# Rounded-float32 matmuls that read their moving operand as two interleaved strands

## The chip, the cores and the metric

One core of a Trainium2 chip runs one program. The metric is the device time in microseconds; the median of three runs is shown, with the span of one profiled execution. The engines are TensorE (PE; its weight loads, PEld, are listed apart), VectorE (DVE), ScalarE (ACT), GpSimd (POOL) and the queue of SyncE (SP), which issues most transfers.

## The reference

Two layers over 512 positions of width 1024, float32. Layer 0 mixes with a Conformer convolution module, layer 1 with native sparse attention; each mixer is followed by a SwiGLU FFN of inner width 2816. The branches of the reference for other mixers do not run at this depth.

```python
D_MODEL = 1024; SEQ = 512; DEPTH = 2; D_FF = 2816

def swiglu_ffn(h, w_in, w_out):
    gate, up = jnp.split(h @ w_in, 2, axis=-1)
    return (jax.nn.silu(gate) * up) @ w_out

def reference(x, ...):
    for i in range(DEPTH):
        h = rmsnorm(x, norm_mix[i])
        if m == 0:   y = conformer_conv_module(h, ...)   # GLU, 31-tap depthwise conv, LayerNorm, SiLU, projection
        elif m == 1: y = nsa_attention(h, ...)           # 16 heads of 64: compressed, selected and window branch
        x = x + y
        h = rmsnorm(x, norm_ffn[i])
        x = x + swiglu_ffn(h, ffn_w_in[i], ffn_w_out[i])
    return x
```

## The kernel before

**Layout.** Activations lie transposed: `x[m]` is a tile of 128 features by 512 tokens (P = 128, T = 512, H = 256), eight of them. A projection multiplies a 128x128 block of weights (stationary, loaded for each matmul) with such a tile (moving, 512 columns) into one PSUM bank.

**Three matmuls a product.** For accuracy each factor is split into a rounded-float32 high part (type `F32R`) and the rounded remainder, and a product is the sum of three matmuls, high by high, high by low and low by high. `mm3` (L320) does that for the projections. ACT makes a high part by a copy that rounds, DVE the low part by a subtraction: `w_hi`/`w_lo` for the weights (tiles `wh`, `wl`), `split_x` (L347) for the activations with the norm's gain (`hh`, `hl`), `divide` and `row_part` for the FFN's inner rows (`ah`, `al`, `row`), `out_parts` for the attention's output (`oh`, `ol`). All of these are stored with the tokens in order and read in order.

**The FFN.** A head of projections over 512 columns is followed by 18 pairs (`pair`) that multiply 2x2 blocks with seven products (Winograd's form) instead of eight: the token axis is halved, so that the moving operands have H = 256 columns. They lie in `ball`, made from `z` by `operand_z`, `operand_t`, `operand_h`, `operand_l`, `operand_th` and `operand_tl` during the head (per chunk of features and per high or low part, 256, 512 and 1024 elements) and later from the FFN's inner rows by `block`. The stationary side is made of sums of weight blocks (`sh`, `sl`, or `wh`, `wl` unsummed). `product` (L1013) issues 12 matmuls for one of the seven products. Then come 14 rows of the second projection in plain form (`row_mm`, 512 columns) and four more pairs (`out_pair`).

**The rest.** The attention's scores (`S`) have keys as the moving operand, 128 to 512 columns wide; the probabilities are transposed by matmuls against an identity in plain float32 (`T<-cc,Pm`) and multiplied with the values (`O<-t,v`, plain float32 too). In the V projection (`v_mm`) the roles are swapped: the tokens `hh`, `hl` are stationary and the weights (304 or 256 columns) are moving. The norms sum squares by matmuls against a column of ones (`ssq`, one column). `warm` (L339) issues bf16 matmuls on zeros while TensorE would wait. The convolution's statistics row `rows` (L679) is read from PSUM through `by_phase`, with a step of eight tokens; the first two key tiles are multiplied into `kr` by `norm_x` (L1752) in another order of tokens, the others (`kraw`) in place.

**Order.** The program's order on each engine is the order in which the code is written, with small parts hung on hooks between matmuls; nearly everything is pinned to it. All instructions of the helper classes carry line 153, so the profile's groups are told apart by tile names.

Of the kernel before, what the change touches and what calls it, by code (L numbers as in the profile page):

```python
# [19 lines left out]
P = 128  # L20
# [142 lines left out]


@with_exitstack
def trunk(ctx: ExitStack, tc: tile.TileContext, A, out):
# [228 lines left out]
    def proj_start(pool, tag, xh, xl, hooks=None, pre=None, into=None):  # L395
# [6 lines left out]
        for i in range(4):  # L402
            wh, wl = next_w()
            for k2 in range(2):
                k = 2 * i + k2
                if pre and k + 1 < NK:
                    pre(k + 1)
                if k == 0 and pre:
                    for w, z in ((wh, xh), (wl, xh), (wh, xl)):
                        for m in range(4):  # L410
                            held(nc.tensor.matmul(pss[m], w[:, m * P:(m + 1) * P], z[0], start=w is wh and z is xh,
                                                  stop=False))
# [25 lines left out]
    def conv_module():  # L438
        acc = new_acc()
        with ExitStack() as cx:  # L440
# [53 lines left out]
            for k in range(NK):  # L494
# [8 lines left out]
                if k == 0:  # L503
                    load_tables()
                    for w, z in ((wh, hh), (wl, hh), (wh, hl)):
                        for m in range(2):
                            held(nc.tensor.matmul(pend[m], w[:, m * P:(m + 1) * P], z[0], start=w is wh and z is hh,
                                                  stop=False))
                    continue
                for m in range(2):  # L510
                    c = slice(k % 2 * 256 + m * P, k % 2 * 256 + (m + 1) * P)
                    for w, z in ((wh, hh), (wl, hh), (wh, hl)):
                        held(nc.tensor.matmul(pend[m], w[:, c], z[k], start=False, stop=z is hl and k == NK - 1))
            for k in range(NK):
# [293 lines left out]
            def ln_mul(i):  # L808
# [5 lines left out]
                ah.append(box["a"][0][:, i, :])  # L814
                for z in (ah[i], lny[i]):
                    pe(nc.scalar.activation(z, vch[i], AF.Silu, scale=v(V_LNG + i), bias=v(V_LNB + i)))

            def ln_low(i):
                al.append(box["a"][1][:, i, :])
                pe(nc.vector.tensor_tensor(al[i], lny[i], ah[i], ALU.subtract))  # L820

# [28 lines left out]
    def ffn(acc, gnext, layer, between=None):  # L850
# [12 lines left out]
        with ExitStack() as cx:  # L863
# [20 lines left out]
            def split_last(part):  # L884
                m, g = NK - 1, v(gcol + NK - 1)
                if part == 0:
                    hh[m] = hps[0].tile([P, T], F32R, tag=f"hh{m}", name=nm(f"hh{m}"))
                    hl[m] = hps[0].tile([P, T], F32R, tag=f"hl{m}", name=nm(f"hl{m}"))
                    nc.scalar.activation(hh[m], x[m], AF.Copy, scale=g)
                else:  # L890
                    nc.vector.scalar_tensor_tensor(hl[m], x[m], g, hh[m], ALU.mult, ALU.subtract)

            ah, al, ys = {}, {}, {}

            def divide(f, pool):
                ah[f] = pool.tile([P, T], F32R, tag=f"ah{f}", name=nm("ah"))
                al[f] = pool.tile([P, T], F32R, tag=f"al{f}", name=nm("al"))
                held(nc.scalar.activation(ah[f], ys[f], AF.Copy))
                held(nc.vector.tensor_tensor(al[f], ys[f], ah[f], ALU.subtract))

# [51 lines left out]
            def operand_h(c):  # L952
                z, zt = ops[c]
                nc.scalar.activation(bh[c][:, :H], z[:, :H], AF.Copy, scale=-1.0)
                nc.scalar.activation(bh[c][:, H:3 * H], z[:, T:], AF.Copy)

            def operand_l(c):
                z, zt = ops[c]
                nc.vector.scalar_tensor_tensor(bl[c][:, :H], z[:, :H], -1.0, bh[c][:, :H], ALU.mult, ALU.subtract)
                nc.vector.tensor_tensor(bl[c][:, H:3 * H], z[:, T:], bh[c][:, H:3 * H], ALU.subtract)  # L960
# [198 lines left out]
            def row_part(f):  # L1159
# [204 lines left out]
    def nsa(acc, cosT, sinT, gnext):  # L1364
# [70 lines left out]
        def qk_bc(C, y2, scale=1.0):  # L1435
# [5 lines left out]
            nc.gpsimd.memset(ys[64:].bitcast(F32), 0.0)  # L1441
            nc.scalar.activation(ys[:64], py[:64], AF.Copy, scale=scale)
            nc.vector.scalar_tensor_tensor(ys[32:64], py[32:64], scale, ys[32:64], ALU.mult, ALU.subtract)
            return ys

        def qk_bcast(c, y):
            bc = p2.tile([P, T], F32, tag="p2", name=nm("bc"))
            pe(nc.tensor.matmul(bc, C["er"][c], y, start=True, stop=True))
            return bc
# [39 lines left out]
        def gain(e, ps):  # L1489
# [15 lines left out]
        def square(e, ps):  # L1505
            sqs[e] = (qk.tile([P, T], F32, tag="q2", name=nm("qsq"), bufs=Q2B) if e in (4, 5) else
                      kp.tile([P, T], F32, tag="qsq", name=nm("qsq"), bufs=SQB))
            nc.scalar.activation(sqs[e], ps, AF.Square)

# [40 lines left out]
        def seq16(t):  # L1550
            return t.rearrange("p (n q) -> p n q", q=16)

        later = []

# [29 lines left out]

        def split_1(q, eng):

            hi, lo = (qk.tile([P, T], F32R, tag="q2", name=nm(z), bufs=Q2B) for z in ("qh", "ql"))
            if eng is nc.scalar:
                eng.activation(hi, q, AF.Copy)
            else:  # L1590
                eng.tensor_copy(hi, q)
            nc.gpsimd.tensor_tensor(lo, q, hi, ALU.subtract)
            return hi, lo

        def k_move(c):
            box["k2", c] = split_1(ks[c], nc.scalar)

# [81 lines left out]
        def q_pair(p):  # L1679
# [46 lines left out]
            def trans():  # L1726
# [4 lines left out]
                pl = q3[1].tile([P, T], F32R, tag="pcl", name=nm("pcl"))  # L1731
                nc.scalar.activation(ph, pt, AF.Copy)
                behind(lambda: nc.vector.tensor_tensor(pl, pt, ph, ALU.subtract))
                pcT[p] = (ph, pl)
# [29 lines left out]
        def v_cmp():  # L1764
            for a in range(2):
                nc.vector.tensor_tensor(to_cmp(1, a), seq16(pss[2 + a]), seq16(R), ALU.mult)
            cmp_move(1)
# [162 lines left out]
        def score(U, t):  # L1930
# [21 lines left out]
            if t == 0:  # L1952
                o, ks = ps[:, :2 * P].rearrange("p (b n) -> p b n", b=2), [z[:, :, :P] for z in ks]
# [43 lines left out]
        def values(Us):  # L1997
# [4 lines left out]
            if br == 1:  # L2002
                ob[j] = (p2, pO)[j % 2].tile([P, T], F32, tag="O", name=nm("O"), bufs=1)
                ph, pl = pcT[j // 2]
                ch, cl = vcb[a, j % 2]
                pe(nc.tensor.matmul(ob[j], ch, ph, start=True, stop=False))
                pe(nc.tensor.matmul(ob[j], ch, pl, start=False, stop=False))
# [11 lines left out]
        def out_parts():  # L2019
            if outs:  # L2020
                j, o = outs.pop()
                h_ = op.tile([P, T], F32R, tag=f"o{j}", name=nm("oh"))
                l_ = oha.tile([P, T], F32R, name=nm("ol"))
                nc.scalar.activation(h_, o, AF.Copy)
                behind(lambda: nc.vector.tensor_tensor(l_, o, h_, ALU.subtract))
                oh.append(h_)
# [180 lines left out]
def _layout(a):  # L2207
# [123 lines left out]
```

## Time and profile before

| | |
|---|---|
| median of three runs (range) | 1156.94 us (1156.37 to 1157.15) |
| profiled execution: its span, first to last instruction | 1156.3 us |
| PE / PEld busy | 1151.0 / 1011.6 us |
| DVE / ACT / POOL busy | 867.4 / 585.1 / 402.6 us |
| instructions on PE | 8341 matmuls, each with a weight load |
| moved by DMA | 164.27 MB, mean 142 GB/s |

No time is listed for the profiled execution beside its span; the span is 0.6 us under the median of the runs. In a row of a group, `out<-in` names the written tile, then the moving and the stationary operand of a matmul, then its rows and columns, the count, and busy time and mean duration of one in ns, and last the idle time before them. `st<-ball,sh 128x256 x1760` are the matmuls of the pairs with summed weights, `pp<-hh,wh 128x512` those of the projections. In an answer by time the first column is the start in us from the span's start, the second the time that the row covers, from the first start to the last end. A row of windows has the stretch, its length, and the busy time of PE, PEld, DVE, ACT and POOL with the number of instructions, then the granted clock, the DMA engines' share and GB/s.

### The profile page before, as it was taken

How to read it: one execution, taken by the hardware profiler on the slowest of the kernel's cores; microseconds unless marked ns; L12 is line 12 of the kernel's file. 1: busy time of each engine (PE TensorE's matmuls, PEld its weight loads, DVE VectorE, ACT ScalarE, POOL GpSimd, SP SyncE). 2: the span in 40 equal slices, each digit the busy share in tenths (PEclk: the TensorE clock that was granted, in tenths of full speed). 3: DMA queues.
4: the chain of work that ended last, by engine and by line, in shares of the span. 5: the costliest groups of instructions: out<-in, count | busy, mean ns of one | idle time of the engine just before them, and what ended most of it. 6: DMA issues, size and time to landing. Idle time of an engine off the chain costs nothing.

```text
span 1156.3 us, 21728 instructions
## 1 busy us (share of the span) xinstructions
PE 1151.0 (100%) x8341; PEld 1011.6 (87%) x8341; DVE 867.4 (75%) x1558; ACT 585.1 (51%) x1118; POOL 402.6 (35%) x441
## 2 busy tenths in 40 slices
PE   9999999999999999999999999999999999999998
PEld 7888788899999988998778877778889999998898
DVE  7898786998777568875676778764699877756566
ACT  6312464565555444454333688763455555544443
POOL 1029122054444101333233577752304444430031
PEclk9999999999999999999999999999999999999999
DMA  9744428278777532534364232112736877762352
GB/s 372 268 124 125 98 91 218 92 195 200 198 192 192 155 119 92 153 104 106 110 160 113 63 75 55 38 38 91 200 109 162 205 198 190 194 184 92 109 128 73
DMA packets 86552, 164.27 MB, mean 142 GB/s; under 512 B 36656, under 2 KB 37808, under 8 KB 85680
## 3 DMA queue, kind: packets, MB, share of 16 engines
q1 hardware_dynamic: 66800, 108.48, 30.9%
q0 software_dynamic: 19504, 54.37, 20.1%
q8 instruction: 65, 1.06, 0.4%
q14 instruction: 39, 0.32, 0.1%
q10 hardware_dynamic: 144, 0.04, 0.0%
HBM read 147.23 MB, written 5.28 MB: 132 GB/s over the span
## 4 chain that ended last, share of the span: by engine, by line
PE 96%; DVE 2%; issue 1%; DMA 1%; ACT 0%; SPq 0%; DVEq 0%; ACTq 0%
PE st L153 50%; PE pp L153 29%; PE O L153 4%; PE S L153 3%; PE T L153 3%; PE pv L153 2%; PE cpe L153 1%; DVE cv L153 1%; PE warm L153 1%; PE psc L153 1%; DVE u L153 0%; DMA swap<-u 0%; PE z L153 0%; PE psq L153 0%; PE rbc L153 0%
## 5 line engine op out<-in xcount | busy, mean ns | idle before, releaser
L153 PE MATMUL st<-ball,sh 128*128 128x256 f32 x1760 | 304.9, 276 | 0.0
L153 PEld LDWEIGHTS st<-ball,sh 128*128 128x128 f32 x1760 | 265.4, 188 | 1.3 <-ACT c L153 1.0
L153 PE MATMUL st<-ball,sl 128*128 128x256 f32 x880 | 242.5, 276 | 0.0
L153 DVE TENSOR_TENSOR wl<-wr,wh 128x1024 fp32r<-128x1024 f32 (+4 forms) x145 | 179.9, 1240 | 83.3 <-ACT wh L153 83.2
L153 ACT ACTIVATE wh<-wr 128x1024 fp32r<-128x1024 f32 (+4 forms) x144 | 148.6, 1032 | 169.0 <-PE st L153 60.2
L153 POOL DMA_DIRECT2D S<-fw_x x88 | 78.3, 890 | 277.0 <-DVE sl L153 221.2
L153 POOL TENSOR_TENSOR S<-S,wr 128x512 f32<-128x512 f32 x84 | 118.2, 1407 | 147.6 <-DMA wr<-fw_op 119.3
L153 PEld LDWEIGHTS st<-ball,sl 128*128 128x128 f32 x880 | 165.3, 188 | 0.0
L153 PE MATMUL pp<-hh,wh 128*128 128x512 f32 x384 | 153.2, 399 | 0.1
L153 PE MATMUL pp<-hh,wl 128*128 128x512 f32 x384 | 149.9, 391 | 0.0
L153 PE MATMUL pp<-hl,wh 128*128 128x512 f32 x384 | 149.6, 390 | 0.0
L153 DVE TENSOR_TENSOR sl<-S,sh 128x512 fp32r<-128x512 f32 x176 | 117.9, 710 | 30.0 <-ACT sh L153 29.1
L153 PE MATMUL st<-ball,wh 128*128 128x256 f32 x704 | 124.1, 276 | 0.0
L153 ACT ACTIVATE sh<-S 128x512 fp32r<-128x512 f32 x176 | 101.0, 621 | 18.5 <-PE st L153 15.0
L153 PE MATMUL st<-row,wh 128*128 128x512 f32 x352 | 108.5, 389 | 0.0
L153 PEld LDWEIGHTS st<-ball,wh 128*128 128x128 f32 x704 | 106.4, 188 | 0.3
L153 PE MATMUL st<-ball,wl 128*128 128x256 f32 x352 | 97.0, 276 | 0.0
L153 PEld LDWEIGHTS pp<-hh,wh 128*128 128x128 f32 x384 | 72.5, 189 | 17.2 <-issue 1.9
L153 POOL TENSOR_SCALAR Pm<-Pm,mx,gates 128x512 f32<-128x512 f32 (+2 forms) x112 | 70.9, 645 | 44.3 <-DVE mx L153 23.2
L153 PEld LDWEIGHTS pp<-hh,wl 128*128 128x128 f32 x384 | 72.4, 189 | 15.5
L153 PEld LDWEIGHTS pp<-hl,wh 128*128 128x128 f32 x384 | 72.2, 188 | 14.5 <-issue 0.2
L153 ACT ACTIVATE c<-st 128x256 f32<-128x256 f32 x132 | 48.6, 377 | 65.2 <-PE st L153 48.7
(267 smaller groups left out, 2173.2 us busy)
## 6 DMA issues: line engine op xcount, KB each, us to landing
S<-fw_x POOLq DMA_DIRECT2D x88, 512.0 KB, 5.9
wr<-fw_in SPq DMA_DIRECT2D x44, 512.0 KB
wr<-fw_or SPq DMA_DIRECT2D x28, 512.0 KB
r<-fw_x SPq DMA_DIRECT2D x44, 256.0 KB
bd<-bands POOLq DMA_DIRECT2D x6, 1280.0 KB, 17.5
wr<-cw_in SPq DMA_DIRECT2D x14, 512.0 KB
wr<-fw_s SPq DMA_DIRECT2D x8, 512.0 KB
wr<-fw_op SPq DMA_DIRECT2D x8, 512.0 KB
```

What stands on the lines that cost most here:

```text
L153: z = f(*a, **kw)
```

## The change

Three views of a row of n columns are added, with `a` the strand (0 or 1) and `b` the place in it. `strands` is how a matmul now reads its moving operand: element 0 of the first half, element 0 of the second half, element 1 of the first half, and so on. `stored` writes a row as two halves, and `source` reads a row with step two, first the even then the odd elements. An operand that is written as `stored` from `source` and read as `strands` comes out in the order of before.

Every matmul whose operands are rounded float32 reads through `strands`: the projections, the FFN's pairs and rows, the V projection, the scores (strands of 64 per 128 keys), the compressed values and the broadcasts of the norms. ACT, DVE and POOL read with step two where they make these operands, and write in one piece. Two places differ. The layer-1 operands (`gcol` is `V_NM1`) stay in order in SBUF, since the V projection needs them as stationary tiles; read as strands, they give PSUM tiles whose columns are permuted, and `gain`, `square` and `v_cmp` read those PSUM tiles with step two. The V weights are permuted on the host. Plain float32 and bf16 matmuls and all weight loads are as before. The number and the order of the instructions on every engine and queue are the same.

```diff
+def strands(z, n=T):
+    return z.rearrange("p (c a b) -> p c b a", a=2, b=n // 2) if n < z.shape[1] else z.rearrange("p (a b) -> p b a", a=2)
+def stored(z, n=T):
+    return z.rearrange("p (c a b) -> p c a b", a=2, b=n // 2) if n < z.shape[1] else z.rearrange("p (a b) -> p a b", a=2)
+def source(z, n=T):
+    return z.rearrange("p (c b a) -> p c a b", a=2, b=n // 2) if n < z.shape[1] else z.rearrange("p (b a) -> p a b", a=2)
...
     def mm3(ps, wh, wl, xh, xl, first, last):
+        xh, xl = strands(xh), strands(xl)
         held(nc.tensor.matmul(ps, wh, xh, start=first, stop=False))
...
         g = v(gcol + m)
-        held(nc.scalar.activation(hh[m], x[m], AF.Copy, scale=g))
-        held(nc.vector.scalar_tensor_tensor(hl[m], x[m], g, hh[m], ALU.mult, ALU.subtract))
+        put, take = (stored, source) if gcol != V_NM1 else (stored, stored)
+        held(nc.scalar.activation(put(hh[m]), take(x[m]), AF.Copy, scale=g))
+        held(nc.vector.scalar_tensor_tensor(put(hl[m]), take(x[m]), g, put(hh[m]), ALU.mult, ALU.subtract))
...
             def operand_th(c):
-                nc.scalar.activation(bh[c][:, 3 * H:], ops[c][1], AF.Copy)
+                nc.scalar.activation(stored(bh[c][:, 3 * H:], H), source(ops[c][1], H), AF.Copy)
             def operand_tl(c):
-                nc.vector.tensor_tensor(bl[c][:, 3 * H:], ops[c][1], bh[c][:, 3 * H:], ALU.subtract)
+                nc.vector.tensor_tensor(stored(bl[c][:, 3 * H:], H), source(ops[c][1], H), stored(bh[c][:, 3 * H:], H),
+                                        ALU.subtract)
...
-                        pe(nc.tensor.matmul(ps[:, :H], p_[:, k], m_[c][:, t], start=first and c == 0 and q == 0,
+                        pe(nc.tensor.matmul(ps[:, :H], p_[:, k], strands(m_[c][:, t], H), start=first and c == 0 and q == 0,
                                             stop=last and c == 3 and q == 2, skip_group_check=True))
...
-                pe(nc.scalar.activation(h_, ys[f], AF.Copy))
-                pe(nc.vector.tensor_tensor(l_, ys[f], h_, ALU.subtract))
+                pe(nc.scalar.activation(stored(h_), source(ys[f]), AF.Copy))
+                pe(nc.vector.tensor_tensor(stored(l_), source(ys[f]), stored(h_), ALU.subtract))
             def block(c, d, e, neg=False):
-                h_, l_ = bh[c][:, d], bl[c][:, d]
+                h_, l_, e = stored(bh[c][:, d], H), stored(bl[c][:, d], H), source(e, H)
...
-            nc.scalar.activation(q, ps, AF.Copy, scale=v(V_KG + e // 2 if e < 6 else V_QG))
+            nc.scalar.activation(stored(q), source(ps), AF.Copy, scale=v(V_KG + e // 2 if e < 6 else V_QG))
...
-                        nc.tensor.matmul(pst[t], l[k][:, tk], r[:, c], start=st and o == 0, stop=sp and o == 2,
+                        nc.tensor.matmul(pst[t], l[k][:, tk], strands(r[:, c], w), start=st and o == 0, stop=sp and o == 2,
                                          skip_group_check=not both)
...
-                o, ks = ps[:, :w], [z[:, br - 1, :w] for z in ks]
+                o, ks = ps[:, :w], [strands(z[:, br - 1, :w], P) for z in ks]
...
-        z = z.reshape(NK, P, VW[hf]).transpose(1, 0, 2)
+        z = z.reshape(NK, P, VW[hf] // 2, 2).transpose(1, 0, 3, 2).reshape(P, NK, VW[hf])
```

The other edits of the diff apply the same three views to the remaining makers and readers (`split_last`, `divide`, `operand_h`, `operand_l`, the convolution's `ah`/`al`, `out_parts`, the compressed probabilities, `qk_bc`, `split_1`).

More of the change, by code (lines that the diff above doesn't have):

```diff
@@ L410, in proj_start @@
                         for m in range(4):
-                            held(nc.tensor.matmul(pss[m], w[:, m * P:(m + 1) * P], z[0], start=w is wh and z is xh,
-                                                  stop=False))
+                            held(nc.tensor.matmul(pss[m], w[:, m * P:(m + 1) * P], strands(z[0]),
+                                                  start=w is wh and z is xh, stop=False))
                 for m in range(4 if k or not pre else 0):
@@ L506, in conv_module @@
                         for m in range(2):
-                            held(nc.tensor.matmul(pend[m], w[:, m * P:(m + 1) * P], z[0], start=w is wh and z is hh,
-                                                  stop=False))
+                            held(nc.tensor.matmul(pend[m], w[:, m * P:(m + 1) * P], strands(z[0]),
+                                                  start=w is wh and z is hh, stop=False))
                     continue
@@ L512, in conv_module @@
                     for w, z in ((wh, hh), (wl, hh), (wh, hl)):
-                        held(nc.tensor.matmul(pend[m], w[:, c], z[k], start=False, stop=z is hl and k == NK - 1))
+                        held(nc.tensor.matmul(pend[m], w[:, c], strands(z[k]), start=False, stop=z is hl and k == NK - 1))
             for k in range(NK):
@@ L814, in ln_mul @@
                 ah.append(box["a"][0][:, i, :])
-                for z in (ah[i], lny[i]):
-                    pe(nc.scalar.activation(z, vch[i], AF.Silu, scale=v(V_LNG + i), bias=v(V_LNB + i)))
+                for z, q in ((stored(ah[i]), source(vch[i])), (lny[i], vch[i])):
+                    pe(nc.scalar.activation(z, q, AF.Silu, scale=v(V_LNG + i), bias=v(V_LNB + i)))
             def ln_low(i):
                 al.append(box["a"][1][:, i, :])
-                pe(nc.vector.tensor_tensor(al[i], lny[i], ah[i], ALU.subtract))
+                pe(nc.vector.tensor_tensor(stored(al[i]), source(lny[i]), stored(ah[i]), ALU.subtract))
             def ln_out(i):
@@ L1441, in qk_bc @@
             nc.gpsimd.memset(ys[64:].bitcast(F32), 0.0)
-            nc.scalar.activation(ys[:64], py[:64], AF.Copy, scale=scale)
-            nc.vector.scalar_tensor_tensor(ys[32:64], py[32:64], scale, ys[32:64], ALU.mult, ALU.subtract)
+            nc.scalar.activation(stored(ys[:64]), source(py[:64]), AF.Copy, scale=scale)
+            nc.vector.scalar_tensor_tensor(stored(ys[32:64]), source(py[32:64]), scale, stored(ys[32:64]), ALU.mult,
+                                           ALU.subtract)
             return ys
@@ L1447, in qk_bcast @@
             bc = p2.tile([P, T], F32, tag="p2", name=nm("bc"))
-            pe(nc.tensor.matmul(bc, C["er"][c], y, start=True, stop=True))
+            pe(nc.tensor.matmul(bc, C["er"][c], strands(y), start=True, stop=True))
             return bc
@@ L1551, in seq16, with halves16 @@
             return t.rearrange("p (n q) -> p n q", q=16)
+        def halves16(t):
+            return t.rearrange("p (a n q) -> p a n q", a=2, q=16)
         later = []
@@ L1583, in ssq, with split_1 @@
                 lead = lead or z
-        def split_1(q, eng):
+        def split_1(q, eng, n=None):
             hi, lo = (qk.tile([P, T], F32R, tag="q2", name=nm(z), bufs=Q2B) for z in ("qh", "ql"))
+            h_, l_, q = (hi, lo, q) if n is None else (stored(hi, n), stored(lo, n), source(q, n))
             if eng is nc.scalar:
-                eng.activation(hi, q, AF.Copy)
+                eng.activation(h_, q, AF.Copy)
             else:
-                eng.tensor_copy(hi, q)
-            nc.gpsimd.tensor_tensor(lo, q, hi, ALU.subtract)
+                eng.tensor_copy(h_, q)
+            nc.gpsimd.tensor_tensor(l_, q, h_, ALU.subtract)
             return hi, lo
         def k_move(c):
-            box["k2", c] = split_1(ks[c], nc.scalar)
+            box["k2", c] = split_1(ks[c], nc.scalar, P)
         def k_stack(c):
@@ L1731, in trans @@
                 pl = q3[1].tile([P, T], F32R, tag="pcl", name=nm("pcl"))
-                nc.scalar.activation(ph, pt, AF.Copy)
-                behind(lambda: nc.vector.tensor_tensor(pl, pt, ph, ALU.subtract))
+                nc.scalar.activation(stored(ph), source(pt), AF.Copy)
+                behind(lambda: nc.vector.tensor_tensor(stored(pl), source(pt), stored(ph), ALU.subtract))
                 pcT[p] = (ph, pl)
@@ L1765, in v_cmp @@
             for a in range(2):
-                nc.vector.tensor_tensor(to_cmp(1, a), seq16(pss[2 + a]), seq16(R), ALU.mult)
+                nc.vector.tensor_tensor(kr[1][:, :, a, :].rearrange("p q (e n) -> p e n q", e=2),
+                                        pss[2 + a].rearrange("p (n q e) -> p e n q", e=2, q=16), halves16(R), ALU.mult)
             cmp_move(1)
@@ L1952, in score @@
             if t == 0:
-                o, ks = ps[:, :2 * P].rearrange("p (b n) -> p b n", b=2), [z[:, :, :P] for z in ks]
+                o, ks = ps[:, :2 * P], [z[:, :, :P].rearrange("p r (a b) -> p r b a", a=2) for z in ks]
             else:
-                o, ks = ps[:, :w], [z[:, br - 1, :w] for z in ks]
+                o, ks = ps[:, :w], [strands(z[:, br - 1, :w], P) for z in ks]
             for i, z in enumerate(ks):
@@ L2005, in values @@
                 ch, cl = vcb[a, j % 2]
+                ph, pl = strands(ph), strands(pl)
                 pe(nc.tensor.matmul(ob[j], ch, ph, start=True, stop=False))
@@ L2023, in out_parts @@
                 l_ = oha.tile([P, T], F32R, name=nm("ol"))
-                nc.scalar.activation(h_, o, AF.Copy)
-                behind(lambda: nc.vector.tensor_tensor(l_, o, h_, ALU.subtract))
+                nc.scalar.activation(stored(h_), source(o), AF.Copy)
+                behind(lambda: nc.vector.tensor_tensor(stored(l_), source(o), stored(h_), ALU.subtract))
                 oh.append(h_)
```

20 lines of the change are left out of this document (11 added, 9 removed).

## The prediction

> **What bounds the kernel now.** I read the page's busy table, then the chain that ended last, then what TensorE waited for, then single stretches of the order of time.
>
> ```profile
> PE 1151.0 (100%) x8341; PEld 1011.6 (87%) x8341; DVE 867.4 (75%) x1558; ACT 585.1 (51%) x1118; POOL 402.6 (35%) x441
> PEclk9999999999999999999999999999999999999999
> PE 96%; DVE 2%; issue 1%; DMA 1%; ACT 0%; SPq 0%; DVEq 0%; ACTq 0%
> PE warm L153 <- DVE zb L153: 1.0, 1, 1.0
> PE cpe L153 <- DMA uf<-swap: 0.4, 1, 0.4
> ```
>
> TensorE is busy for 1151.0 of 1156.3 us at full granted clock, it is 96% of the chain, and its longest wait on anybody is 1.0 us. So the time is the sum of the distances from one matmul's start to the next (the pitch), and an edit is worth what it does to the pitch. A matmul's own duration in the profile (276 or 390 ns) includes its drain and overlaps the next one; pitches come from starts.
>
> ```profile
> 404.09 0.39 PE L153 MATMUL st<-ah,wh 128*128 128x512 f32 x1
> 414.97 0.62 PE L153 MATMUL st<-row,wh 128*128 128x512 f32 x2
> 299.84 0.28 PE L153 MATMUL st<-ball,sl 128*128 128x256 f32 x1
> 305.96 0.28 PE L153 MATMUL st<-ball,sl 128*128 128x256 f32 x1
> 134.31 0.38 PE L153 MATMUL warm<-zb 128*128 128x512 bf16 x1
> 135.62 1.89 PE L153 MATMUL warm<-zb 128*128 128x512 bf16 x8
> ```
>
> From 404.09 to 414.97 stand 48 rounded-float32 matmuls of 512 columns: 10.88 / 48 = 0.2267 us each. From 299.84 to 305.96 stand 54 of 256 columns: 6.12 / 54 = 0.1133. The second is half of the first, 0.443 ns a column at either width, so the cost sits in the columns and not in a fixed part of each instruction. Eight bf16 matmuls of 512 columns, in the same array at the same clock, take (1.89 - 0.38) / 7 = 0.2157. The array can therefore pass a column in 0.421 ns; the float32 stream, with twice the bytes per column, gets one in 0.443. What is short by 5% is the feeding of the moving operand, and it is short by the same share in every float32 product of this kernel.
>
> **The change part by part.** No instruction is added, removed or moved on any engine, no wait is new, and the transfers keep their sizes (the host permutes one weight table). Three things differ: the address order in which the moving operand is read, the step with which ACT, DVE and POOL read when they make the operands, and, where the PSUM columns come out permuted, the step with which it is read.
>
> *512 columns.* The groups below give the counts; a product is three matmuls, so `oh` stands for 192 and `ah` for 144.
>
> ```profile
> L153 PE MATMUL pp<-hh,wh 128*128 128x512 f32 x384 | 153.2, 399 | 0.1
> L153 PE MATMUL pp<-a,wh 128*128 128x512 f32 x128 | 39.1, 391 | 0.0
> L153 PE MATMUL pp<-oh,wh 128*128 128x512 f32 x64 | 25.0, 391 | 0.0
> L153 PE MATMUL st<-row,wh 128*128 128x512 f32 x352 | 108.5, 389 | 0.0
> L153 PE MATMUL st<-ah,wh 128*128 128x512 f32 x48 | 18.7, 390 | 0.0
> L153 PE MATMUL S<-kh,St 128*128 128x512 f32 x32 | 15.2, 475 | 0.0
> ```
>
> 1152 (`hh`, `hl`) + 192 (`a`) + 192 + 528 (`row`: 352 and half as many) + 144 + 64 (`S`, from `kh` and `kl`) = 2272. The trace of before has no float32 moving operand with a step, so the new pitch is bounded: below by the bf16 row, 0.2157, which is the array's own rate; above by twice the time per column, as the float32 transposes below show it. I take the lower end. The loss is a fixed share of the columns, as of a single stream that pauses each time it passes some piece of its addresses, and two streams a kilobyte apart can hide one's pause behind the other. 2272 x (0.2267 - 0.2157) = 25.0 us.
>
> *256 columns.* Here another floor comes into sight, the weights.
>
> ```profile
> L153 PE MATMUL st<-ball,sh 128*128 128x256 f32 x1760 | 304.9, 276 | 0.0
> L153 PE MATMUL st<-ball,sl 128*128 128x256 f32 x880 | 242.5, 276 | 0.0
> L153 PE MATMUL st<-ball,wh 128*128 128x256 f32 x704 | 124.1, 276 | 0.0
> L153 PE MATMUL st<-ball,wl 128*128 128x256 f32 x352 | 97.0, 276 | 0.0
> 22.19 0.86 PEld L153 LDWEIGHTS ssq<-ones,acc 128*128 128x128 f32 x7
> 22.96 0.19 PEld L153 LDWEIGHTS pp<-hh,wh 128*128 128x128 f32 x1
> 226.50:397.00 170.50, 170.49 (x1500) 170.07 (x1499) 135.73 (x200) 94.22 (x178) 76.99 (x69) 1.00 0.77 194
> ```
>
> Where a matmul has one column, the pitch is that of its weight loads: seven in 0.86 us, with 0.19 for one, is (0.86 - 0.19) / 6 = 0.1117 us. Every matmul here has its own 128x128 float32 weights, and in the pair stage (226.5 to 397, columns PE, PEld, DVE, ACT, POOL) the load port is busy 170.07 of 170.50. So a 256-column matmul can fall from 0.1133 to 0.1117 and no further: 3696 x 0.0016 = 5.9 us. If the weights were no floor it would reach half of the bf16 pitch, 0.1079, or about 20 us in all; that is a rival below.
>
> The Trainium skill ("TensorE: Matmul & The Clock Gate", Back-to-back issue gap) gives a warm pitch of N / 2.4 + 2.5 ns. That is 215.8 at 512 columns, which the bf16 rows agree with and the float32 rows (226.7) do not; at 256 it is 109.2, and an estimate by that page would make this term 3696 x 4.1 ns = 15 us, where the weight loads of this trace allow 5.9.
>
> *The rest.*
>
> ```profile
> L153 PE MATMUL pv<-wh,hh 128*128 128x304 f32 x32 | 9.8, 307 | 0.0
> L153 PE MATMUL S<-kh,St 128*128 128x256 f32 x48 | 15.0, 314 | 0.0
> ```
>
> Three times 32 matmuls of 304 columns and as many of 256 in the V projection, twice 48 scores at 256 and 64 at 384 gain between 2 and 8 ns each in the proportion of these two pitches; with some 40 broadcasts and compressed values of 512 columns I put them at 1.5 us together.
>
> *Making the operands.* Writes stay contiguous; reads get a step of two elements. ACT:
>
> ```profile
> L153 ACT ACTIVATE rows<-lnst 128x512 f32<-128x512 f32 x1 | 0.6, 579 | 0.0
> L153 ACT ACTIVATE qa<-psq 128x512 f32<-128x512 f32 x3 | 1.8, 599 | 4.8 <-PE psq L153 4.8
> L153 DVE TENSOR_TENSOR kr<-kraw,bc 128x512 f32<-128x512 f32 x2 | 2.0, 1086 | 0.9 <-PE bc L153 0.9
> L153 DVE TENSOR_TENSOR kraw<-kraw,bc 128x512 f32<-128x512 f32 x4 | 2.6, 681 | 0.0
> L153 DVE TENSOR_TENSOR ball<-z,ball 128x1024 fp32r<-128x1024 f32 x8 | 9.8, 1224 | 1.2 <-ACT ball L153 1.2
> L153 DVE TENSOR_TENSOR ball<-z,ball 128x512 fp32r<-128x512 f32 x8 | 5.5, 685 | 0.0
> L153 DVE SCALAR_TENSOR_TENSOR ball<-z,ball 128x256 fp32r<-128x256 f32 x8 | 3.4, 419 | 0.0
> 181.10:226.30 45.20, 45.20 (x208) 37.67 (x207) 39.94 (x64) 22.59 (x32) 3.97 (x4) 1.00 0.58 164
> 820.00:866.00 46.00, 45.90 (x210) 37.95 (x210) 40.20 (x64) 23.77 (x33) 5.32 (x6) 1.00 0.57 163
> ```
>
> `rows` reads PSUM with a step of eight elements (`by_phase`) and takes 579 ns, `qa` reads it in order and takes 599: a step costs ACT nothing there, and I take zero. For DVE the nearest rows are the same product written with a large step (`kr`, 1086 ns) and in order (`kraw`, 681): the bounds are 0 and 0.41 us per 512 elements. I take 0, since only reads change, by a step of 8 bytes; the upper end counts in the range. The cover is thinnest in the heads of the two FFNs (windows 181 and 820): DVE, the third of the columns, 39.94 of 45.20 us, with PE to become 43.1 (192 matmuls, 2.1 less). The three `ball` rows make 4 x (1024 + 512 + 256) = 7168 operand elements in each head; at the upper end these cost 14 x 0.41 = 5.7 us, put DVE at 45.6 and make each head 2.5 us longer than forecast; with the kernel's first eight splits (8 x 0.41 = 3.3 us) about 8 us in all. At the lower end DVE still ends inside PE's time. For work that now just fits and then does not, I take off 1 us.
>
> The sum: 25.0 + 5.9 + 1.5 - 1 = 31.4 us. From the profiled span of 1156.3, 1124.9; the median of the runs shown is 1156.94, 0.6 above the span, so 1125.5, and I say **1125**.
>
> **The rivals.**
>
> *More than that.* The weights are no floor: the loads measured are those of plain float32, and the loads of rounded float32 may be shorter. For it: today's pitch of 0.1133 is the feeding's own, so nothing shows the weights binding yet. Then the 256-column term is 16 to 20 us instead of 5.9: about 1112.
>
> *Half of it.* The two strands start at equal places of their pieces (they lie 1024 or 512 bytes apart) and pause together, so half of the pauses stay: 12.5 us at 512 columns, 0.1106 at 256 and so still the floor, 5.9, together with the rest 19: 1138. Nothing in the profile speaks for or against it.
>
> *No effect.* The feeding is limited in bytes per time, whatever their order: 4 bytes in 0.443 ns against bf16's 2 in 0.421. Then only DVE's cost is left, 0 to 8 us, of which most is covered while PE stays slow: 1157. Against it: a plain limit of bytes has no reason to lie within 5% of the array's own rate, while a short pause after every so many columns gives just such a share.
>
> *Slower.* The reader fetches a piece of several elements and keeps one; now each element lies in another piece than the one before it, and each piece is fetched again and again. The place is every float32 product; the price, by the nearest rows, is that of the float32 transposes:
>
> ```profile
> 659.22 0.60 PE L153 MATMUL T<-cc,Pm 128*128 128x128 f32 x4
> L153 PE MATMUL T<-cc,Pm 128*128 128x128 f32 x304 | 44.6, 275 | 0.2
> ```
>
> (0.60 - 0.275) / 3 = 0.108 us for 128 columns, 0.85 ns a column, which is 0.43 and 0.217 for the two widths: 2272 x 0.207 + 3696 x 0.104 + some 25 = 880 us more, about 2040. It decides from the first nanosecond, since TensorE has no slack: a pitch above 0.2267 is a loss. Against it: ACT's stepped read in PSUM was free, and a reader that holds two pieces is enough.
>
> The Trainium skill speaks for this rival ("Advanced Engine Details and Errata", SBUF Cachelines): SBUF has lines of 16 bytes, a reader has full speed while it stays on a line, needs two hits on each, and pays where every access goes to another. By that rule the strands, whose neighbours are never on one line, run slower and the order of before is the best one; yet the order of before, four hits on each line, already falls short of the array by 5%, which the rule does not tell of. No row here reads a moving operand with a step.
>
> **How the numbers follow.** Forecast (1118 to 1131): 0.45. More: 0.17. Half: 0.12. No effect: 0.09. Slower: 0.17. A measurement of this kernel tells 0.2%, about 2.3 us, from no change. So faster is 0.45 + 0.17 + 0.12 = 0.74, same 0.09, slower 0.17. The range leaves out the slower case and the far end of the first rival: 1108 (both widths at the array's rate) to 1158 (no effect); the likeliest case's own is 1118 to 1131.
>
> **What would show it.** The pitch of 512 columns in the rows of the FFN falls from 0.2267 to 0.2157; that of 256 columns to 0.1117, with the load port as its partner in step (0.108 would mean the first rival, 0.1133 none). TensorE stays without waits, DVE's `ball` and `hl` rows and ACT's keep their durations, and DVE in the heads stays below TensorE's time. A 512-column pitch above 0.2267 makes the forecast wrong at once; one between 0.216 and 0.226 is the half case; DVE rows longer by 0.1 us or more with PE waiting in the heads would put the result above 1130.

## The result and the profile after

The changed kernel takes **1139.35 us** (median of four, 1138.75 to 1140.02) against 1157.05 for the kernel before: a ratio of 0.985, with a 95% interval from 0.983 to 0.986. That is 17.7 us less, where 31.4 were forecast. Its profiled execution has a span of 1137.0 us against 1156.3, 19.3 less. Where a run lists both, its time is about 1.8 us longer than its span. So the span of 1156.3 fits the longest of the four executions before (1158.10), while 1137.0 belongs to the shortest after (1138.75), and the difference of the medians, 17.7, is the better figure.

First the page after, the busy table and the chain that ended last, and what TensorE waited for (total us, times, longest):

```profile
PE 1121.3 (99%) x8341; PEld 1005.1 (88%) x8341; DVE 880.7 (77%) x1558; ACT 610.8 (54%) x1118; POOL 402.9 (35%) x441
PE 82%; DVE 9%; ACT 4%; issue 3%; DMA 1%; POOL 1%; SPq 1%; DVEq 0%; POOLq 0%; ACTq 0%
PE pp L153 <- DVE wl L153: 5.0, 6, 1.2
PE bc L153 <- DVE kcb L153: 1.2, 1, 1.2
```

TensorE is busy for 29.7 us less, and the span is 19.3 us shorter: the difference is idle time that was not there. DVE and ACT, which were 2% of the chain together, are 13% of it, and TensorE now waits for `wl`, the low parts of the weights. DVE and ACT themselves are busy for 13.3 and 25.7 us more.

The pitches, in the order of time (start, time covered): `row` with 512 columns, every third matmul of it, and the pairs with 256.

```profile
423.11 0.38 PE L153 MATMUL st<-row,wl 128*128 128x512 f32 x1
428.29 0.38 PE L153 MATMUL st<-row,wl 128*128 128x512 f32 x1
301.26 0.28 PE L153 MATMUL st<-ball,sl 128*128 128x256 f32 x1
303.27 0.28 PE L153 MATMUL st<-ball,sl 128*128 128x256 f32 x1
```

24 matmuls from 423.11 to 428.29: 0.2158 us each (0.2267 before; 0.2157 was forecast). 18 from 301.26 to 303.27: 0.1117 (0.1133 before; 0.1117 was forecast). Both are the forecast to the third digit, and still 13.7 us of the gain are missing.

The groups that make the operands, ACT's first, from the same profile:

```profile
L153 ACT ACTIVATE ball<-z 128x1024 fp32r<-128x1024 f32 x8 | 13.0, 1619 | 13.9 <-DVE z L153 13.9
L153 ACT ACTIVATE row<-y 128x512 fp32r<-128x512 f32 x22 | 18.8, 863 | 0.0
L153 ACT ACTIVATE qraw<-pp,vec 128x512 f32<-128x512 f32 x8 | 5.5, 689 | 23.6 <-PE pp L153 23.6
L153 DVE TENSOR_TENSOR ball<-z,ball 128x1024 fp32r<-128x1024 f32 x8 | 12.3, 1538 | 3.1 <-ACT ball L153 3.1
L153 DVE TENSOR_TENSOR row<-y,row 128x512 fp32r<-128x512 f32 x22 | 18.2, 836 | 0.0
L153 DVE TENSOR_TENSOR ol<-O,oh 128x512 fp32r<-128x512 f32 x8 | 5.5, 685 | 4.3 <-ACT oh L153 4.3
```

In the kernel before the same groups read:

```profile
L153 ACT ACTIVATE ball<-z 128x1024 fp32r<-128x1024 f32 x8 | 8.5, 1061 | 14.7 <-DVE z L153 14.7
L153 ACT ACTIVATE row<-y 128x512 fp32r<-128x512 f32 x22 | 13.3, 614 | 0.0
L153 ACT ACTIVATE qraw<-pp,vec 128x512 f32<-128x512 f32 x8 | 5.5, 690 | 24.9 <-PE pp L153 24.9
L153 DVE TENSOR_TENSOR row<-y,row 128x512 fp32r<-128x512 f32 x22 | 14.9, 684 | 0.0
L153 DVE TENSOR_TENSOR ol<-O,oh 128x512 fp32r<-128x512 f32 x8 | 5.5, 686 | 4.3 <-ACT oh L153 4.3
```

In the changed kernel the rows that read SBUF with step two take longer: a `row` of 512 costs ACT 0.25 us more (614 to 863; 1061 to 1619 for 1024) and DVE 0.15 more (684 to 836; 1224 to 1538). Over ACT's groups of 512 in the FFNs this goes from 0.17 (`ah`, 624 to 792) to 0.30 us (`ball<-y`, 616 to 915). The rows that read PSUM with step two (`qraw`, `ol`) cost nothing more. The experiments below show that the step alone is not the reason.

What that does shows in an FFN head, here a stretch of DVE's and ACT's own order of time in the changed kernel, and the first matmul behind it (idle time and its releaser in brackets):

```profile
195.74 1.60 ACT L153 ACTIVATE ball<-z 128x1024 fp32r<-128x1024 f32 x1 [1.77 <-DVE z L153]
196.04 0.83 DVE L153 TENSOR_TENSOR ball<-z,ball 128x512 fp32r<-128x512 f32 x1
197.37 1.53 DVE L153 TENSOR_TENSOR ball<-z,ball 128x1024 fp32r<-128x1024 f32 x1 [0.50 <-ACT ball L153]
198.82 1.40 DVE L153 SCALAR_TENSOR_TENSOR z<-x,vec,Rb 128x512 f32<-128x512 f32 x2
200.14 1.22 DVE L153 TENSOR_TENSOR wl<-wr,wh 128x1024 fp32r<-128x1024 f32 x1
201.41 0.48 PE L153 MATMUL pp<-hh,wl 128*128 128x512 f32 x1 [1.19 <-DVE wl L153]
```

ACT's copy of 1024 lasts until 197.34, DVE stands idle for it for 0.50 us, then needs 1.53 for the low part of it, 1.40 for the next chunk's `z`, and only then comes to the `wl` that stands behind them in its order. TensorE stands still for 1.19 us for that `wl`. It is no single late instruction but a loop: DVE makes `z`, ACT rounds it, DVE subtracts, and the weights' low part is queued in the middle.

One round of that loop, from one `wl` to the next with the same instructions between them, before (the first two rows, and the first matmul that reads the second `wl`) and after (the start of the round that ends at 200.14):

```profile
196.76 1.22 DVE L153 TENSOR_TENSOR wl<-wr,wh 128x1024 fp32r<-128x1024 f32 x1
203.09 1.22 DVE L153 TENSOR_TENSOR wl<-wr,wh 128x1024 fp32r<-128x1024 f32 x1
205.22 0.39 PE L153 MATMUL pp<-hh,wl 128*128 128x512 f32 x1
```

```profile
192.97 1.22 DVE L153 TENSOR_TENSOR wl<-wr,wh 128x1024 fp32r<-128x1024 f32 x1
```

A round took 6.33 us and takes 7.17. Of the 0.84 more, DVE's own three `ball` rows make 0.5 and its longer wait for ACT (0.50 against 0.19) makes 0.3. Before, the `wl` of 203.09 was ready at 204.31, 0.91 us ahead of its first matmul. A faster TensorE uses up a `wl`, which serves 24 matmuls, in 5.18 instead of 5.44 us, and so eats into that lead from the other side.

One count by stage of all this, from the starts of the same matmuls in both profiles (us; "by pitch" is the number of its rounded-float32 matmuls times the pitches' differences of 0.0109 and 0.0016):

| stage | before | after | gain | by pitch |
|---|---|---|---|---|
| conv output projection | 43.72 | 43.12 | 0.6 | 2.1 |
| FFN head, the first / the second | 45.40 / 46.03 | 46.00 / 46.60 | -0.6 / -0.6 | 2.1 / 2.1 |
| pairs, the first / the second FFN | 175.49 / 175.87 | 174.95 / 175.39 | 0.5 / 0.5 | 2.6 / 2.6 |
| FFN rows, each | 72.79 | 69.28 | 3.5 | 3.5 |
| attention's output projection | 43.42 | 41.33 | 2.1 | 2.1 |

Where nothing else is in the way, the gain is what the pitch says; in the heads, where `ball` is made, it turned into a loss.

### The profile page after: what moved, and what is told of

It reads as the page before. It is cut to its first block, busy times and chain, and to the rows that moved or that the text cites. A ratio compares the mean times of both kernels' runs of the same rounds, so it can differ in the third digit from the quotient of the medians.

```text
span 1137.0 us, 21733 instructions
## 1 busy us (share of the span) xinstructions
PE 1121.3 (99%) x8341; PEld 1005.1 (88%) x8341; DVE 880.7 (77%) x1558; ACT 610.8 (54%) x1118; POOL 402.9 (35%) x441
## 4 chain that ended last, share of the span: by engine, by line
PE 82%; DVE 9%; ACT 4%; issue 3%; DMA 1%; POOL 1%; SPq 1%; DVEq 0%; POOLq 0%; ACTq 0%
PE st L153 47%; PE pp L153 18%; PE O L153 4%; PE T L153 3%; PE S L153 3%; PE cpe L153 3%; DVE wl L153 2%; DVE z L153 2%; PE pv L153 2%; ACT ball L153 1%; ACT wh L153 1%; PE psc L153 1%; DVE c L153 1%; DVE g L153 0%; DMA x<-xT 0%
## 5 line engine op out<-in xcount | busy, mean ns | idle before, releaser
L153 PE MATMUL st<-ball,sh 128*128 128x256 f32 x1760 | 301.6, 276 | 2.1 <-DVE t L153 0.8
L153 DVE TENSOR_TENSOR wl<-wr,wh 128x1024 fp32r<-128x1024 f32 (+4 forms) x145 | 177.6, 1225 | 64.6 <-ACT wh L153 64.2
L153 PEld LDWEIGHTS st<-ball,sl 128*128 128x128 f32 x880 | 168.9, 192 | 0.8 <-DVE sl L153 0.8
L153 PE MATMUL pp<-hh,wl 128*128 128x512 f32 x384 | 146.4, 382 | 5.0 <-DVE wl L153 5.0
L153 PE MATMUL pp<-hh,wh 128*128 128x512 f32 x384 | 148.7, 388 | 0.1
L153 PE MATMUL pp<-hl,wh 128*128 128x512 f32 x384 | 145.4, 379 | 0.0
L153 PE MATMUL st<-row,wh 128*128 128x512 f32 x352 | 104.7, 379 | 0.0
L153 ACT ACTIVATE g<-g 128x512 f32<-128x512 f32 x44 | 27.8, 632 | 99.4 <-DVE g L153 99.4
```

Source lines behind the costliest of these rows:

```text
L153: z = f(*a, **kw)
```

## The experiments

### Reading alone and making alone

The change does two things that can be taken apart. Theory A: the reads with step two in SBUF cost the missing 13.7 us. Theory B: ACT and DVE could not have followed a faster TensorE anyway. The first run keeps the strands and makes operands in order:

```diff
 def source(z, n=T):
-    return z.rearrange("p (c b a) -> p c a b", ...) if n < z.shape[1] else z.rearrange("p (b a) -> p a b", a=2)
+    return stored(z, n)
```

> Strands are read as in the change, but ACT, DVE and POOL make the operands in order and read PSUM in order: no read with step two is left, and every product's columns come out permuted (that reordering of the tokens is what this kernel leaves out). Theory A, the step-two reads in SBUF (ball 1061 to 1619 ns on ACT, 1224 to 1538 on DVE) gave back about 13 us: pitches 0.2157 and 0.1117 as in the change and the whole gain, 1126 (1123 to 1130). Theory B, ACT and DVE could not follow a faster TensorE even with the operand making of before: within 3 us of the change, 1137 to 1142.

Measured: 1129.97 us, ratio 0.977 (0.975 to 0.979), at pitches of 0.2158 and 0.1117. Theory B is out: with the operand making of before and the faster reading, 9.4 us come back. Theory A's number was 1126, and the upper end of its interval is met; the last 4 us are not the step-two reads. Between the two profiled executions the difference is 8.9 us. By the starts of the same matmuls, 4.5 of them lie in the two FFN heads, 2.6 in the pairs behind them, 1.3 at the start of the kernel, where the first splits are, and 1.0 in the convolution's output projection; all other stages together differ by -0.5.

The second run keeps the stepped making and reads in order:

```diff
 def strands(z, n=T):
-    return z.rearrange("p (c a b) -> p c b a", ...) if n < z.shape[1] else z.rearrange("p (a b) -> p b a", a=2)
+    return stored(z, n)
```

> The operands are stored and PSUM is read as in the change, but every matmul reads its operand in one piece (the columns come out permuted; the reordering is left out). Both theories: pitches back at 0.2267 and 0.1133. Theory A: the step-two reads cost something even under the slower TensorE, above all in the FFN heads, 1158 to 1163. Theory B: they are covered, 1156 to 1158.

Measured: 1157.27 us, ratio 1.000 (0.999 to 1.001): nothing, and A's expectation for it was wrong. Its window over the first FFN head, and the same 210 matmuls in the kernel before (columns: stretch, length, then busy time of PE, PEld, DVE, ACT, POOL):

```profile
180.30:225.70 45.40, 45.40 (x210) 37.82 (x209) 40.17 (x64) 23.44 (x33) 3.93 (x4) 1.00 0.58 164
```

```profile
181.13:226.53 45.40, 45.40 (x210) 37.86 (x208) 40.17 (x64) 22.62 (x33) 3.94 (x4) 1.00 0.59 165
```

45.40 us both times. The same groups of operand making, in this run:

```profile
L153 ACT ACTIVATE ball<-z 128x1024 fp32r<-128x1024 f32 x8 | 9.2, 1144 | 14.5 <-DVE z L153 14.5
L153 ACT ACTIVATE row<-y 128x512 fp32r<-128x512 f32 x22 | 14.2, 655 | 0.0
L153 DVE TENSOR_TENSOR ball<-z,ball 128x1024 fp32r<-128x1024 f32 x8 | 9.8, 1224 | 1.6 <-ACT ball L153 1.6
L153 DVE TENSOR_TENSOR row<-y,row 128x512 fp32r<-128x512 f32 x22 | 14.9, 684 | 0.0
```

They read SBUF with the same step as in the change, and yet DVE's rows are as short as in the kernel before (684, 1224) and ACT's are 0.04 us longer for 512 elements (614 to 655), not 0.25. In the first of these two runs, where TensorE read strands and the operands were made in order, they were short too (613 for ACT's `row`, 684 for DVE's). So the operands are dear only where both meet: a read of SBUF with step two while TensorE reads strands. The changed kernel shows it inside its first head, in two copies of 512 elements from `z` to `ball`, one beside running matmuls and one in the 1.19 us in which TensorE stands still:

```profile
193.08 0.89 ACT L153 ACTIVATE ball<-z 128x512 fp32r<-128x512 f32 x1
200.25 0.67 ACT L153 ACTIVATE ball<-z 128x512 fp32r<-128x512 f32 x1
```

The faster reading is worth 27.1 us with operands made in order, the stepped making alone costs nothing, and together they are worth 17.7: the 9.4 us are in neither edit alone, because neither alone has the dear rows. Why the two kinds of reads disturb each other is open.

### The change without the pairs

`ball` is made and read in order, everything else is as in the change.

```diff
-    pe(nc.tensor.matmul(ps[:, :H], p_[:, k], strands(m_[c][:, t], H), ...
+    pe(nc.tensor.matmul(ps[:, :H], p_[:, k], m_[c][:, t], ...
 # operand_h, operand_l, operand_th, operand_tl and block: no stored, no source
```

> The change without its part in the FFN's pairs: ball is made in order and read in order, so the 256-column products keep 0.1133 and give up 5.9 us; the heads lose 14 step-two reads each on ACT and on DVE. Theory A: the heads get back their 2.7 us each and the pairs what they lost, the two nearly cancel, 1138 (1135 to 1141). Theory B: only the loss, 1143 to 1147.

Measured: 1138.73 us, ratio 0.984 (0.983 to 0.986), A's number. Its first head:

```profile
179.74:223.47 43.73, 43.57 (x210) 37.85 (x209) 39.27 (x63) 21.94 (x31) 4.33 (x5) 1.00 0.59 169
```

Without the stepped `ball` the head takes 43.73 instead of 46.00 us, so its loss was that operand's and no other's. The pairs pay for it: 176.16 against 174.95 us. In the change, the 256-column part comes to nothing within the scatter of the runs (1137.53 to 1140.26 here).

This run also shows the price of the step switching with what TensorE reads. `ah` is made with step two in both rows; at 222.48 TensorE runs the head's last projections, which read strands, and at 246.11 the pairs, which here read `ball` in order:

```profile
222.48 0.89 ACT L153 ACTIVATE ah<-y 128x512 fp32r<-128x512 f32 x1
246.11 0.66 ACT L153 ACTIVATE ah<-y 128x512 fp32r<-128x512 f32 x1
```

### The step put where it is free

All operands of the projections and the FFNs stay in order in SBUF, but for the attention's output, which is made from PSUM as in the change. Their products come out of PSUM permuted, and each instruction that reads PSUM undoes it with step two, as the change already does for its layer-1 projections:

```diff
-        put, take = (stored, source) if gcol != V_NM1 else (stored, stored)
+        put, take = stored, stored
...
-                nc.vector.tensor_tensor(g, pG, box["R"], ALU.mult)
+                nc.vector.tensor_tensor(stored(g), source(pG), stored(box["R"]), ALU.mult)
...
-                pe(nc.scalar.activation(t, ps[:, :H], AF.Copy))
+                pe(nc.scalar.activation(stored(t), source(ps[:, :H]), AF.Copy))
...
-                pe(nc.vector.tensor_tensor(x[m], x[m], pss[m], ALU.add))
+                pe(nc.vector.tensor_tensor(stored(x[m]), stored(x[m]), source(pss[m]), ALU.add))
```

and so for the other readers of PSUM in the convolution's gate and output, the pairs and the halves of the output.

> All products read strands; operands stay in order in SBUF (but for the keys, the compressed probabilities and the attention output, as in the change), so PSUM comes out permuted and whoever reads it does so with step two, as the change does for its layer-1 projections. The same result as the reference's. PSUM rows were not slower with step two in the change (qraw 690 and 689, ol 686 and 685). Theory A: the whole gain, 1127 (1123 to 1131). Theory B: as the change, 1137 to 1142.

Measured: **1130.64 us**, ratio 0.977 (0.976 to 0.979). It is 8.7 us faster than the change and 26.5 faster than the kernel before, and level with the run that left the order out. Its first head and first pairs:

```profile
175.89:219.62 43.73, 43.57 (x209) 37.86 (x208) 39.11 (x63) 21.87 (x31) 4.20 (x5) 1.00 0.59 169
219.62:393.29 173.67, 173.18 (x1528) 172.06 (x1527) 137.68 (x203) 95.93 (x182) 77.10 (x69) 1.00 0.75 192
```

43.73 against 46.00 and 173.67 against 174.95. The rows that now read PSUM with step two, beside matmuls that read strands, take what they took in the kernel before: 681 ns for `x<-x,st` and 686 for `g<-pp,Rb`, both of 512 columns on DVE. This is the version to keep.

### Which floor holds 256 columns

In the run that reads strands and makes operands in order, 11 of a product's 12 matmuls load half of their weights:

```diff
+    w_ = P if c + q == 0 else P // 2
-    pe(nc.tensor.matmul(ps[:, :H], p_[:, k], ...
+    pe(nc.tensor.matmul(ps[:w_, :H], p_[:, k.start:k.start + w_], ...
```

> The run that reads strands and makes operands in order, with one more edit: of the 12 matmuls of a product in the FFN's pairs, 11 load and use 64 weight columns instead of 128 (half of their outputs, and the tokens' order, are left out). The moving side is the same. If the weight loads hold the 256-column pitch at 0.1117, it falls to the array's own rate, 0.1079 to 0.109, and the time by 3696 x 11/12 x 0.003 = 9 to 13 us, 1117 to 1121. If it is the moving side, 0.1117 stays and the time is 1128 to 1131.

Measured: 1122.34 us in one run. The same group of matmuls in it, 18 from the first row to the second:

```profile
300.94 0.27 PE L153 MATMUL st<-ball,sl 128*64 128x256 f32 x1
302.91 0.27 PE L153 MATMUL st<-ball,sl 128*64 128x256 f32 x1
```

1.97 / 18 = 0.1094. The time is 7.6 us under the run that it builds on and 1.3 above the range expected for it; the pitch decides between the two. The moving side did not change, so 0.1117 was not its floor, and the first rival (1112, the weights no floor) is out. The edit halves the rows written to PSUM along with the weights, and no run parts these two; for the weight loads speaks that matmuls of one column have the same 0.1117.

### Which order of reading is fast, and why

Six orders, all with operands made in order. Theory P: one stream pauses as it passes from piece to piece of its addresses, and a second one hides it; that is what the prediction assumed. Theory Q: neighbours clash when they are read one right after the other. Only the last view of `strands` differs:

```diff
-    z.rearrange("p (a b) -> p b a", a=2)              # 0, 256, 1, 257, ...
+    z.rearrange("p (b a) -> p a b", a=2)              # r1: 0, 2, 4, ..., then 1, 3, 5, ...
+    z.rearrange("p (a b k) -> p b a k", a=2, k=4)     # r2: 0 to 3, 256 to 259, 4 to 7, ...
+    z.rearrange("p (g a b) -> p g b a", a=2, b=8)     # r3: 0, 8, 1, 9, ..., 7, 15, then 16, 24, ...
+    z.rearrange("p (a b) -> p b a", a=4)              # r4: 0, 128, 256, 384, 1, 129, ...
+    z.rearrange("p (g a b) -> p g b a", a=2, b=2)     # r5: 0, 2, 1, 3, then 4, 6, 5, 7, ...
+    z.rearrange("p (a b k) -> p b a k", a=2, k=2)     # r6: 0, 1, 256, 257, 2, 3, ...
```

> As the run that reads strands and makes operands in order, but each rounded-float32 product (scores aside) reads the even elements of its row and then the odd ones (step of 8 bytes); the tokens' order is left out. Theory P, a pause each time one stream passes from one piece of some 64 bytes to the next: twice as many pieces are passed, a 512-column pitch of about 0.240. Theory Q, elements that are neighbours in memory clash when they are read one right after the other: 0.2157, as with strands.

> As before, but read as pieces of 4 neighbouring elements (16 bytes) taken in turn from the two halves; the tokens' order is left out. Theory P: the two halves still hide each other's pauses, 0.2157. Theory Q: three of four steps go to a neighbour, so the pitch stays near that of plain reading, 0.224 to 0.2267.

> As before, but the two strands lie 8 elements (32 bytes) apart inside each group of 16 (64 bytes), so that the groups are passed one after the other as in plain reading; the tokens' order is left out. Theory P: as plain reading, 0.2267. Theory Q: 0.2157.

> As before, but four strands, each a quarter of the row; the tokens' order is left out. Theory P: 0.2157 if four pieces can be held, above 0.2267 if only two can. Theory Q: 0.2157.

The rows of each run, 24 matmuls of 512 columns from the first to the second. Step two:

```profile
803.04 0.63 PE L153 MATMUL st<-row,wl 128*128 128x512 f32 x1
813.87 0.63 PE L153 MATMUL st<-row,wl 128*128 128x512 f32 x1
```

Pieces of four:

```profile
467.15 0.41 PE L153 MATMUL st<-row,wl 128*128 128x512 f32 x1
473.15 0.41 PE L153 MATMUL st<-row,wl 128*128 128x512 f32 x1
```

Strands 32 bytes apart:

```profile
418.10 0.38 PE L153 MATMUL st<-row,wl 128*128 128x512 f32 x1
423.28 0.38 PE L153 MATMUL st<-row,wl 128*128 128x512 f32 x1
```

Four strands:

```profile
516.17 0.45 PE L153 MATMUL st<-row,wl 128*128 128x512 f32 x1
522.97 0.45 PE L153 MATMUL st<-row,wl 128*128 128x512 f32 x1
```

Pitches of 0.451, 0.250, 0.2158 and 0.283 us (whole kernels, one run each: 2104.9, 1255.0, 1130.9 and 1376.5). P fails on the first three: step two is far above its 0.240, strands 32 bytes apart pass from piece to piece one after the other like plain reading and are still fast, and two far streams in pieces of four are slower than plain. Q fails on step two, which never reads neighbours and is by far the slowest, on four strands, and on pieces of four, which are slower than plain reading. What does agree is a number: plain reading and step two cost 0.2267 / 128 = 1.77 and 0.451 / 256 = 1.76 ns per 16 bytes passed, whether four or two elements of them are used. From that a third theory, L: a line of 16 bytes costs 1.77 ns if lines come singly, and less if two are open at once. Against it S: an inner pattern of two elements with a step is what matters, wherever they lie.

> Order 0, 2, 1, 3 within each group of four elements (16 bytes), then the next group; the tokens' order is left out. Plain reading and step two agree on one number: 0.2267 / 128 = 1.77 ns and 0.451 / 256 = 1.76 ns per 16-byte line passed, whether four or two of its elements are used. Theory L, a line costs 1.77 ns when lines come one after another and less when two are open at once: here one line is open, 0.2267. Theory S, only the inner pattern of two elements with a step matters: 0.2157.

> Pairs of neighbours (8 bytes) taken in turn from the two halves; the tokens' order is left out. Theory L: two lines are open at once, as with strands, 0.2157. Theory S: no inner step, 0.2267 or above.

The order 0, 2, 1, 3 within 16 bytes:

```profile
427.19 0.39 PE L153 MATMUL st<-row,wl 128*128 128x512 f32 x1
432.63 0.39 PE L153 MATMUL st<-row,wl 128*128 128x512 f32 x1
```

Pairs from the two halves in turn:

```profile
598.12 0.51 PE L153 MATMUL st<-row,wl 128*128 128x512 f32 x1
606.12 0.51 PE L153 MATMUL st<-row,wl 128*128 128x512 f32 x1
```

0.2267 and 0.333 (1155.6 and 1587.6 us). With one line open, the pattern with a step is as slow as plain reading: S is out. But two lines open with two elements taken from each in turn is slower than plain, not fast: L is out as it stood. What the runs show is a list, not a mechanism: of eight orders only single elements from two streams, near or far, reach 0.2158. Why pairs and fours from the same two streams lose what single elements gain stays open.

## Why the prediction was right and where it was not

**The time.** 1139.35 lies inside the range of 1108 to 1158 and above the likeliest case's own, 1118 to 1131. Of the 13.7 us that are missing, 9.4 came with the making of the operands, where 1 had been taken off, and 5.3 were missing without it.

**What bounds the kernel.** Right. TensorE had no slack, the pitch was the time, and the stages with nothing else in them (rows, the attention's output) gained 3.5 and 2.1 us as counted.

**512 columns, "I take the lower end".** Right in size: 0.2158 against 0.2157. The reason given, two streams that hide each other's pauses, fell: strands 32 bytes apart do as well and two streams in pieces of four do not.

**256 columns, "0.1117 and no further".** Right in size, and in cause as far as the halved weights can show it. By the estimate from the Trainium skill ("TensorE: Matmul & The Clock Gate", Back-to-back issue gap) the pitch would have been 109.2 ns; the section gives its formula for an isolated matmul and says that it leaves out the weight load. Halved weights give about that, 109.4, and with full weights the trace has 111.7.

**Making the operands.** This is the step that failed: "a step costs ACT nothing there, and I take zero", "for DVE I take 0", and "I take off 1 us". Taken alone, the zeros were nearly right: with stepped reads and no strands, DVE's rows cost nothing more and ACT's 0.04 us per 512 elements. But they were priced from a trace in which no matmul reads strands, and the parts of the change were added up as if they did not touch each other. While TensorE reads strands, ACT pays 0.17 to 0.30 us per 512 elements read from SBUF and DVE 0.15, inside the bounds given for DVE (0 to 0.41) and outside the zero given for ACT, whose row was a read of PSUM. The term that was put at 1 us measured 9.4 (1139.35 less 1129.97).

The test of the cover failed too. The prediction looked at DVE's busy time against TensorE's in the head; by that sum, 14 rows at 0.15 us put DVE at 42.0 us, inside TensorE's 43.1, and nothing is lost. After the change DVE is busy for 40.36 of 46.00 us there, and TensorE waits all the same:

```profile
177.12:223.12 46.00, 43.76 (x209) 37.85 (x208) 40.36 (x61) 24.19 (x29) 4.32 (x5) 1.00 0.57 161
```

What counts there is the loop from DVE to ACT and back, with `wl` queued inside it: a round grew by 0.84 us, some 0.3 of it through ACT, which had no bound in the prediction, and the lead of `wl` was gone. The head became 2.3 us longer than with operands in order, near the 2.5 of the prediction's upper end, but by chance: that had DVE alone, at 0.41. The heads hold 4.5 of the 8.9 us between the two profiled executions; how the pairs, the start and the convolution lose theirs was not followed. The prediction's own sign for this case came out as written: DVE rows longer by 0.1 us or more, TensorE waiting in the heads, and a time above 1130.

**The cover without it.** Even with operands at their old price 27.1 of the 32.4 us before deductions arrived. The stage counts of that run put the missing part in the pairs (1.8 instead of 2.6 in each FFN), the query and key projections (69.45 us became 67.92, where the pitch alone promised 2.6), the heads (1.7 instead of 2.1 each), the convolution's output projection (1.6 instead of 2.1) and the attention. The longest waits of TensorE that this run has and the kernel before has not are for DVE and ACT (`kcb` 1.2 us, `t` 0.6, `gates` 0.5), so the cover was thin also at the old price. No run took those waits away one by one.

**The rivals.** "Half of it" forecast 1138 and the time is 1139, by chance: its pitches (0.2212 and 0.1117) are not the ones measured. "More" fell with the weights, "no effect" with the pitch. "Slower" did not happen with two strands, but a price of that size exists for another order: step two runs at 0.451 a matmul and 2105 us a kernel, where the rival had 0.43 and 2040 from the float32 transposes. The rule weighed there, from the Trainium skill ("Advanced Engine Details and Errata", SBUF Cachelines), says that a line needs at least two hits and that going to another line each time is dear. The four strands bear the second out (0.283). The rest does not: step two has two hits on each line and half the speed, and two strands, of which no two neighbours share a line, are the only kind of order that reaches the array's rate.

## What to carry to other kernels

Price a stepped access by the memory that it reads and by what else reads that memory at the same time. Here a read of SBUF with step two cost DVE nothing and ACT 0.04 us per 512 float32 while the matmuls read in order, and 0.15 and 0.17 to 0.30 while they read strands; from PSUM it was free for both. So a permutation that a matmul's operand needs belongs behind the matmul, at the PSUM read, and two edits that are each harmless have to be tried together. Before a stream is made faster, follow the longest loop between the other engines beside it, with all that is queued in it, rather than their busy shares: 88% busy was enough to stop TensorE. And where an operand's order is free, try several on the chip: orders that look alike ran from 0.2158 to 0.451 us a matmul.

## What the runs showed of the hardware

- A rounded-float32 moving operand read in order passes 512 columns in 0.2267 us, and as two strands of single elements in 0.2158, near or far apart. Pieces of four take 0.250, four strands 0.283, pairs 0.333, step two 0.451.
- Reads of SBUF with step two by ACT and DVE slow down while TensorE reads two strands: for 512 elements 614 to 863 ns on ACT and 684 to 836 on DVE. With the same reads and the matmuls in order they take 655 and 684, and with strands and reads in order 613 and 684. From PSUM neither slows, also beside strands (690 and 689, 686 and 685).
- With 128 weight columns a 256-column matmul as strands went at 0.1117 us, the pitch of one-column matmuls with such weights; with 64 it goes at 0.109.
